# Rotary embedding: the first batch is stored in transfers of 8, 8 and 16 KB rows instead of four of 8 KB rows

## The chip, the core and the metric

The kernel runs on one core of a Trainium2 chip. The time is the device time of one execution in microseconds (us). The kernel before took 163.35 us, the median of three runs (163.34 to 163.67).

## What is computed

```python
x: [8, 2048, 8, 64] float32          # batch, sequence, heads, head dimension
cos, sin: [2048, 32] float32
x1, x2 = x[..., :32], x[..., 32:]
out1 = x1 * cos - x2 * sin           # cos, sin broadcast over batch and heads
out2 = x1 * sin + x2 * cos
out  = concatenate([out1, out2], axis=-1)
```

Each batch is 4 MB of input and 4 MB of output. With the two tables of 256 KB each, about 67.6 MB pass between HBM and SBUF.

## The kernel before

**Tiles.** The 2048 positions of a batch lie on 128 partitions, 16 positions on each, so one batch is one tile `xt` of 128 rows of 32 KB (`ROW` = 8192 floats). `UNIT` is a quarter of that, 2048 floats or 8 KB of each row. There are five such tiles (`NBUF = 5`); batches 5, 6 and 7 reuse the tiles of batches 0, 1 and 2. The result is written over the input in the same tile, and the tile is stored from there.

**Loads.** All loads of `x` are issued by SyncE (SP) in `load`, lines 64 to 70. Batch 0 comes in three transfers, with rows of 8, 8 and 16 KB; every other batch in one transfer with rows of 32 KB. The loads of batches 0 to 4 are issued at the start. The load of batch b+5 (line 193) stands behind the work of batch b and waits until every store of batch b has landed, because it overwrites that tile. Below, x0 to x7 are the loads of the batches.

**Stores.** `store`, lines 72 to 74, issues them on ScalarE's queue (ACT), for the last batch on SP's. `shares`, lines 177 to 182, says how a batch is cut into stores: batch 0 into four with rows of 8 KB (below s0a to s0d), batches 1 to 6 into one each (s1 to s6, rows of 32 KB), and the last batch into rows of 16, 8 and 8 KB (s7a to s7c). The loop at the end issues a store as soon as the pieces that it covers have been rotated.

**Arithmetic.** `rotate` works on pieces of `UNIT` floats of a row (the first and last of the work on half of that). In a piece of kind A, GpSimd (POOL) makes `t2` from the swapped halves and the sine table in two multiplications (line 122), VectorE (DVE) makes `t1` from `xt` and the cosine table (line 129) and adds both into `xt` (line 136). In the first pieces of batches 1 to 5 (kinds B and C) the addition is done by TensorE as two matmuls with the identity into PSUM, and ScalarE copies the sum into `xt` (lines 145, 165). In kind C, DVE also makes `t2` (line 148).

**What sets the order.** The order on each engine is that of the program (`keep_in_program_order`). On the two DMA queues that matter, q1 carries what SP issues and q10 what ACT issues. Each transfer announces its landing on one of eight semaphores that are handed out in turn, so a transfer may also have to wait for the landing of the one that had the same semaphore before it.

Of the kernel before, what the change touches and what calls it, by code (L numbers as in the profile page):

```python
# [10 lines left out]
def kernel(  # L11
# [18 lines left out]
    UNIT = 4 * HD  # L30
# [145 lines left out]

    def shares(b):
        if b == 0:
            return [UNIT] * 4
        if b == last:  # L180
            return [2 * UNIT, UNIT, UNIT]
        return [ROW]

    for b in range(B):
        done = 0
        outs = list(spans(shares(b)))
        for lo, n in spans(pieces(b)):
            rotate(b, lo, n)
            done = lo + n
            while outs and sum(outs[0]) <= done:  # L190
                store(b, *outs.pop(0))
        if b + NBUF <= last:
            load(b + NBUF)
# [30 lines left out]
```

## Time and profile before

| what | value |
|---|---|
| median of three runs | 163.35 us |
| the profiled execution, its own time | 164.17 us |
| its span, first to last instruction | 162.4 us |
| DVE busy | 140.1 us (86% of the span) |
| POOL busy | 138.8 us (85%) |
| PE, ACT busy | 49.1 us (30%), 12.8 us (8%) |
| DMA, moved in all | 67.65 MB, 417 GB/s over the span |
| q1, q10: share of the 16 DMA engines' time | 55.1%, 42.5% |

The profile is of one execution, 0.82 us above the median of the runs; 1.8 us of its time lie outside the span. Busy shares are of the whole span. In the digits by slice, each digit is a fortieth of the stretch shown, in tenths of full use, 9 being 90% or more. A transfer is spread over the 16 DMA engines: its 128 rows give 8 rows to each, and a record of a few bytes that marks the landing follows them on each engine. "To landing" is the time from a transfer's issue until the last of those marks.

### The profile page before, as it was taken

What the parts mean: (1) busy time and instruction counts of PE and PEld (TensorE: products, weight loads), DVE (VectorE), ACT (ScalarE), POOL (GpSimd) and SP (SyncE); (2) the same over time, 40 slices, a digit from 0 to 9 for tenths busy, and PEclk for the clock granted to TensorE, in tenths of its full rate; (3) what the DMA queues carried; (4) which work ended last, traced back from release to release, by engine and by line L of the source; (5) the groups of instructions that cost most, each with busy time, mean ns of one, the idle gap of its engine ahead of it and who ended that gap; (6) DMA issues with size and microseconds to landing.
All of it is one profiled execution on the core that took longest, in us unless ns stands there. A gap on an engine that the chain in (4) does not pass through costs nothing.

```text
span 162.4 us, 462 instructions
## 1 busy us (share of the span) xinstructions
PE 49.1 (30%) x80; PEld 18.5 (11%) x80; DVE 140.1 (86%) x66; ACT 12.8 (8%) x14; POOL 138.8 (85%) x70
## 2 busy tenths in 40 slices
PE   0000000597209750977058805971000000000000
PEld 0000000233003210322022302230000000000000
DVE  0397999999999999999999999999999999999300
ACT  3300000002200220022001120022000000000000
POOL 1499997999999999999995999999999999993000
PEclk9999999999965997589857995699555555555555
DMA  5999799899899899989999999899999999999992
GB/s 182 426 426 517 337 470 452 363 476 460 353 478 468 349 474 476 396 388 509 388 388 501 404 438 460 388 460 438 396 476 420 396 484 412 396 460 428 396 428 113
DMA packets 3602, 67.65 MB, mean 417 GB/s; under 512 B 400, under 2 KB 400, under 8 KB 656
## 3 DMA queue, kind: packets, MB, share of 16 engines
q1 hardware_dynamic: 2016, 38.01, 55.1%
q10 hardware_dynamic: 1584, 29.62, 42.5%
q14 instruction: 2, 0.02, 0.0%
HBM read 34.08 MB, written 33.55 MB: 417 GB/s over the span
## 4 chain that ended last, share of the span: by engine, by line
DVE 75%; POOL 9%; issue 6%; DMA 3%; DVEq 0%
DVE t L129 40%; DVE xt L136 33%; POOL t L122 9%; DMA sin_sb<-in_sin_dram 3%; DVE t L148 3%; DVEq L136 0%
## 5 line engine op out<-in xcount | busy, mean ns | idle before, releaser
L122 POOL TENSOR_TENSOR t<-xt,sin_sb 128x1024 f32<-128x1024 f32 (+1 forms) x32 | 70.7, 2210 | 8.2 <-DMA sin_sb<-in_sin_dram 5.0
L129 DVE TENSOR_TENSOR t<-xt,cos_ps 128x2048 f32<-128x2048 f32 (+1 forms) x34 | 73.4, 2166 | 0.8
L122 POOL TENSOR_TENSOR t<-xt,nsin 128x1024 f32<-128x1024 f32 (+1 forms) x32 | 70.7, 2211 | 0.0
L136 DVE TENSOR_TENSOR xt<-t,t 128x2048 f32<-128x2048 f32 (+1 forms) x29 | 62.2, 2145 | 4.2 <-POOL t L122 1.2
L143 PE MATMUL o<-t,eye 128*128 128x512 f32 x24 | 16.9, 794 | 23.2 <-DVE t L129 19.7
L160 PE MATMUL o<-t,eye 128*128 128x512 f32 x16 | 12.0, 842 | 37.6 <-DVE t L129 35.4
L144 PE MATMUL o<-t,eye 128*128 128x512 f32 x24 | 14.9, 709 | 0.0
L145 ACT COPY xt<-o 128x1024 f32<-128x1024 f32 x6 | 6.1, 1012 | 45.7 <-PE o L144 34.9
L143 PEld LDWEIGHTS o<-t,eye 128*128 128x128 f32 x24 | 5.6, 257 | 32.6 <-issue 26.7
L160 PEld LDWEIGHTS o<-t,eye 128*128 128x128 f32 x16 | 3.7, 257 | 43.1 <-issue 39.2
L165 ACT COPY xt<-o 128x1024 f32<-128x1024 f32 x4 | 4.0, 1012 | 47.7 <-PE o L161 47.7
L144 PEld LDWEIGHTS o<-t,eye 128*128 128x128 f32 x24 | 5.6, 235 | 8.0 <-issue 7.5
L93 DVE COPY cos_ps<-cos_sb 128x512 f32<-128x512 f32 x1 | 0.7, 695 | 6.8 <-DMA cos_sb<-in_cos_dram 6.8
L161 PE MATMUL o<-t,neye 128*128 128x512 f32 x8 | 6.2, 870 | 0.2
L148 DVE TENSOR_TENSOR t<-xt,sin_ps 128x2048 f32<-128x2048 f32 x2 | 4.6, 2280 | 0.0
L161 PE MATMUL o<-t,eye 128*128 128x512 f32 x8 | 4.1, 593 | 0.0
L161 PEld LDWEIGHTS o<-t,neye 128*128 128x128 f32 x8 | 2.1, 294 | 5.2 <-issue 3.6
L161 PEld LDWEIGHTS o<-t,eye 128*128 128x128 f32 x8 | 1.5, 190 | 1.9 <-issue 1.9
L90 ACT ACT_TABLE_LOAD x1 | 1.3, 1283 | 1.2 <-PEq L208 1.2
L90 ACT ACTIVATE nsin<-sin_sb 128x512 f32<-128x512 f32 x1 | 0.6, 629 | 3.9 <-DMA sin_sb<-in_sin_dram 3.9
L91 ACT COPY sin_ps<-sin_sb 128x512 f32<-128x512 f32 x1 | 0.6, 579 | 0.0
L80 POOL MEMSET eye<- 128x128 f32 x1 | 0.2, 206 | 0.3 <-POOLq L208 0.3
(6 smaller groups left out, 1.0 us busy)
## 6 DMA issues: line engine op xcount, KB each, us to landing
xt<-in_x_dram SPq DMA_DIRECT2D x7, 4096.0 KB, 27.9
out_dram<-xt ACTq DMA_DIRECT2D x6, 4096.0 KB, 34.0
out_dram<-xt ACTq DMA_DIRECT2D x4, 1024.0 KB, 26.5
xt<-in_x_dram SPq DMA_DIRECT2D x2, 1024.0 KB, 6.5
xt<-in_x_dram SPq DMA_DIRECT2D x1, 2048.0 KB, 12.0
out_dram<-xt SPq DMA_DIRECT2D x1, 2048.0 KB, 14.6
out_dram<-xt SPq DMA_DIRECT2D x2, 1024.0 KB, 10.9
sin_sb<-in_sin_dram ACTq DMA_DIRECT2D x1, 256.0 KB, 5.5
```

Source lines behind the costliest of these rows:

```text
L90: keep(nc.scalar.mul(nsin, sin_sb, -1.0))
L93: keep(nc.vector.tensor_copy(cos_ps, cos_sb))
L122: nc.gpsimd.tensor_mul(out=t2u[:, :, u, :].rearrange("p (r h) d -> p r h d", h=H), in0=xu[:, :, 1 - u, :].rearrange("p (r h) d -> p r h d" ...
L129: nc.vector.tensor_mul(out=t1.rearrange("p (r k d) -> p r k d", r=nr, d=Dh), in0=xk, in1=rep(cos_ps[:, r0 : r0 + nr, :], 2 * H),)
L136: keep(nc.vector.tensor_add(out=xt, in0=t1, in1=t2))
L143: nc.tensor.matmul(oc, eye, t1[:, cs], start=True, stop=False)
L144: nc.tensor.matmul(oc, eye, t2[:, cs], start=False, stop=True)
L145: keep(nc.scalar.copy(xt[:, 2 * j * C : 2 * (j + 1) * C], o))
L148: nc.vector.tensor_mul(out=t2.rearrange("p (r k d) -> p r k d", r=nr, d=Dh), in0=xk, in1=rep(sin_ps[:, r0 : r0 + nr, :], 2 * H),)
L160: nc.tensor.matmul(oc, eye, t1u[:, gs, u, :], start=True, stop=False)
L161: nc.tensor.matmul(oc, eye if u else neye, t2u[:, gs, 1 - u, :], start=False, stop=True)
L165: nc.scalar.copy(xu[:, :, u, :], o.rearrange("p (g d) -> p g d", d=Dh))
```

## The change

The third and the fourth quarter of batch 0 are stored by one transfer. It has 128 rows of 16 KB, is issued when the last piece of batch 0 is done, and carries 2 MB. The first two quarters are stored as before. Nothing else in the source changes.

```diff
     def shares(b):
         if b == 0:
-            return [UNIT] * 4
+            return [UNIT, UNIT, 2 * UNIT]
         if b == last:
             return [2 * UNIT, UNIT, UNIT]
         return [ROW]
```

In the built program ACT has one DMA instruction fewer: two stores of 128x2048 and one of 128x4096 stand where four of 128x2048 stood. The instructions of PE, DVE, POOL and SP, their order and their shapes are the same. As there is one transfer fewer, the semaphores that announce landings are handed out differently from there on. The load x2 then waits for the landing of the sine table instead of that of the first part of x0, x3 for the cosine table instead of the second part of x0, and x4 for the third part of x0 instead of the first store of batch 0.

## The prediction, made before the changed kernel was run

> **What bounds the kernel now.** I began with the page's rows by engine and by slice, because DVE (86%) and DMA both look full.
>
> ```profile
> span 162.4 us, 462 instructions
> ...
> DMA  5999799899899899989999999899999999999992
> ...
> DMA packets 3602, 67.65 MB, mean 417 GB/s; under 512 B 400, under 2 KB 400, under 8 KB 656
> ```
>
> The DMA digits are high from the second slice to the last but one. To see whether 9 means full, I asked for one stretch, from the first packet (1.7) to where DMA thins out (159.2); the last two columns are DMA share and GB/s.
>
> ```profile
> 1.70:159.20 157.50, 49.15 (x80) 18.53 (x80) 140.11 (x66) 12.22 (x14) 138.11 (x64) 0.77 1.00 429
> ```
>
> The share is 1.00: the 16 DMA engines never pause for 157.5 us. DVE in the same stretch is busy 140.1, and its last addition ends at 151.9, 10 us before the end. So the end is set by bytes, not by arithmetic. The tail shows by how much the DMA engines differ:
>
> ```profile
> DMA  8999995988999895331111111010100000000000
> ```
>
> Each digit is 0.135 us. At 159.2 nearly all engines are done; the ones are one or two engines that run on. Chaining the trace's packets engine by engine gives last ends of 159.2 to 159.8 on fourteen engines (median of all 16: 159.3), 160.64 on one and 161.13 on one. The span ends 1.2 us behind that last packet. The late engine carries the same rows; seven of its 32 KB rows took 1.28 to 1.72 us instead of 1.21, all between 66 and 125 us, and the second late one had an 8 KB instruction fetch of 0.31 followed by a row 0.54 too long.
>
> Next, who shares the engines while batch 0 is stored (42 to 62 us):
>
> ```profile
> q1 hardware_dynamic: 231, 6.52, 75.7%
> q10 hardware_dynamic: 245, 1.88, 22.2%
> ```
>
> Packets 231 to 245, bytes 3.5 to 1: an engine takes one row from each queue in turn, whatever its size. A store row of 8 KB gets one turn against a load row of 32 KB. Last, SP's waits and the issue of x5:
>
> ```profile
> SPq L67 <- DMA out_dram<-xt: 88.1, 4, 33.6
> ```
>
> ```profile
> 63.03 0.33 SPq L67 DMA_DIRECT2D xt<-in_x_dram  x1
> ```
>
> SP waits 33.6 us for batch 0's stores: s0d, issued at 27.6, needs 35.3 to land (62.9), and x5 goes out at 63.03.
>
> **The change, part by part.** I sum against the profiled execution (164.17, which is 0.82 above the median) and subtract the same from the median.
>
> *Saved transfer time.* In the packet records a row of 8 KB takes 0.309, of 16 KB 0.611, of 32 KB 1.213 us. Per engine, 8 x (2 x 0.309 - 0.611) = 0.056, and one landing mark fewer, 0.009: together 0.065 us off an engine that is never idle, so this counts in full. [...]
>
> *The ACT issue removed* (0.34 us) costs nothing: ACT next works at 36.78, and the joint store goes out at 27.6.
>
> *The third quarter waits longer*, from 22.9 to 27.6. That is covered by q10's own backlog: the first rows of the four stores run at 17.1, 29.4, 41.6 and 53.7, every 8 x (1.213 + 0.309) = 12.2 us, so until 41.6 the queue has s0a and s0b to serve. Were it empty, the 4.7 us would show (third rival).
>
> *The new semaphore order* moves the issue of x3 from 9.3 to about 6.8 and of x4 from 28.9 to about 14.2 (landings 6.7 and 14.1), and of x2 from 6.1 to 6.3. Their rows run at 37.7, 49.8 and 25.4, one load behind the other on q1, so all are issued long before their turn: nothing.
>
> *The joint store.* From 41.6 its 8 rows alternate with 8 load rows: 8 x (1.213 + 0.611) = 14.6, to 56.2; with the mark and its way about 56.8. Batch 0's tile is free 6.1 us earlier than 62.9, and SP issues x5 at about 57 instead of 63. But q1 is then not empty. Of x3 and x4, 8 rows pass in those 14.6 us (in the profile nearly 10), and 5 rows of x4 are left. They now alternate with s1's 32 KB rows: 5 x 2.43 = 12.1, to about 68.5. There x5 begins, where in the profile it began at 67.1. Between 61.6 and 67.1 q1 was empty in the profile, and s1 had the engines alone; that gap is filled, no bytes are gained. From there on both queues stay full, loads are one pair of rows (2.4 us) later than before and stores one pair earlier:
>
> x5 lands at 87.0 + 2.4 = 89.4; POOL wants it at 97.05. x6 lands at 106.7 + 2.4 = 109.1; wanted at 110.79. x7 lands at 126.3 + 2.4 = 128.7; wanted at 129.05. s1 and s2 land at about 76.4 and 96.7 instead of 78.8 and 99.1, so x6 and x7 are issued earlier, which changes nothing, as they queue behind x5 and x6. The thinnest cover is x7's:
>
> ```profile
> 129.05 2.32 POOL L122 TENSOR_TENSOR t<-xt,sin_sb 128x1024 f32<-128x1024 f32 x1
> ```
>
> If x7 is d late for that, POOL's pair of operations ends at 133.65 + d, and DVE adds at 134.96: 1.3 more. If DVE slips too, the last store (issued at 151.9) still has the engines' backlog: its first row runs at 156.7, and by the nearest row, s7a's 3.8 us from issue to first row, it could be issued 1.0 later. So 0.35 + 1.3 + 1.0 = 2.6 us cover x7, and I charge nothing.
>
> *The lag of the slowest engine* is the unknown. It was 161.13 - 159.3 = 1.8 us and grew where load rows of 32 KB alternate with store rows of 32 KB. From below: without it the end is 159.8, the next engine's, so up to 1.4 us are to be won. From above: 29 load rows per engine now meet 32 KB store rows instead of 24 (the five of x4 join), which scaled gives 1.8 x 29/24 = 2.2, or +0.4; one more fetch of the observed kind on the late engine would add 0.31 + 0.54. I take 0, since neither seed of the lag is visibly removed or doubled for certain, and keep -1.4 to +0.85 for the range.
>
> Sum: 164.17 - 0.065 + 0 = 164.1 for the profiled execution, 163.35 - 0.065 = 163.3 for the median.
>
> **Rivals.** A measurement of this kernel can tell about 0.2% (0.33 us) from no change, so "same" is 163.02 to 163.68.
>
> *Slower: the lag grows.* The stretch of 32 KB against 32 KB rows lengthens as above. For: all but one of the late engine's long rows fell in that stretch, three of them right behind a store's landing mark, and one more such mark (s0c's) now falls among loads. Against: the marks at 28, 40 and 52 us, between 8 KB store rows, left the next load row at its usual length. It decides when the late engine gains over 0.4 us; with +0.4 to +0.85 the time is 163.7 to 164.2.
>
> *Faster: the lag shrinks.* The late engine's first long row (0.22 too long) ran at 66.2, the last before x5 came up on the empty queue. That restart vanishes. If that engine then keeps step, the other one is last: 160.64 - 161.13 = -0.5, or 162.8; if both do, -1.4, or 161.9. Against: the restart as cause rests on one row.
>
> *Slower: the joined store starts late and pushes x5, x6, x7.* The third store's 4.7 us are then paid: x5 first at 71.7, x7 landing at 130.9, 1.9 behind POOL's wish, 0.6 left for DVE, and at most that at the end: 163.9 at worst. It needs an empty q10 at 22.9, where s0b was issued at 18.2 and took 22.8 to land, so it has 3 in 100. [...]
>
> *The usual hope, that x5's earlier issue speeds the kernel,* is in my sum: x5 starts later, not earlier.
>
> **The numbers.** No change 0.37; lag grows 0.30 and late store 0.03, so slower 0.33; lag shrinks 0.30. The likeliest is no change, 163.3 (163.0 to 163.7 by itself). The range leaves out about 1 in 10 on each side: below, the case where both late engines keep step; above, a lag grown by more than 0.85: 162.5 to 164.2.
>
> **What would show it.** Right: DMA share 1.00 up to about 159; s0c lands near 56.8; x5 is issued near 57 but lands near 89, later than before; x7 near 128.7; s1 near 76.4; DVE ends at 151.9. Wrong: a gap in the DMA share, x5 landing before 87, POOL waiting for x7 by over 2.6 us, or last packet ends that differ from 161.1 while the median engine stays at 159.3, which would put the change into the lag.

## The result and the profile after

In 20 runs each the changed kernel took 163.40 us (163.29 to 163.53) and the kernel before 164.14 (163.34 to 165.46): ratio 0.996, interval 0.9945 to 0.9974. It is 0.4% faster, a little over the 0.2% that I had called the bound. The three runs known beforehand (median 163.35) lay at the low end of a wide spread; the profiled execution of before, 164.17, was the typical one. The change narrows the spread from 2.1 to 0.24 us, and takes the median down to near the best that the kernel before reached.

The page and the same stretch as before (its last two columns are DMA share and GB/s), both of the changed kernel:

```profile
span 161.5 us, 460 instructions
...
DMA  5999998998999999999999999999999999999994
...
DMA packets 3458, 67.65 MB, mean 419 GB/s; under 512 B 384, under 2 KB 384, under 8 KB 640
```

```profile
1.70:159.40 157.70, 49.24 (x80) 18.53 (x80) 140.11 (x66) 12.22 (x14) 138.22 (x64) 0.77 1.00 429
```

The same bytes, the same full share, the same DVE time. What differs is the end. DMA share from 157 us on after the change, each digit 0.135 us; the same row of the kernel before, shown in the prediction, reaches six digits further, with eleven digits from 1 to 3 behind its fall where this one has three (1, 2, 1): a few of the sixteen engines were still at work there:

```profile
DMA  7795959898594979851020100000000000000000
```

The median DMA engine ends at 159.33 before and at 159.52 after, so the common work got no shorter. (In the profile after, the rows of x1 already ran 0.25 us later at 15 us, before any store.) The last engine ends at 161.13 before and at 160.36 after: 0.77 of the 0.82 us between the two profiled executions (164.17 and 163.35). Measured from the median engine, the last one lags by 1.80 us before and by 0.84 after. In all profiles of this study the whole time is the last engine's end plus 2.9 to 3.2 us, so these last ends stand for the times.

The steps in the middle are there much as worked out. The queues from 42 to 62 us (packets, MB, share of the engines), SP's waits, the issue of x5, and POOL's first operation on x7:

```profile
q1 hardware_dynamic: 176, 5.24, 61.8%
q10 hardware_dynamic: 177, 3.42, 39.8%
```

```profile
SPq L67 <- DMA out_dram<-xt: 79.0, 4, 26.9
```

```profile
55.98 0.33 SPq L67 DMA_DIRECT2D xt<-in_x_dram  x1
```

```profile
129.43 2.32 POOL L122 TENSOR_TENSOR t<-xt,sin_sb 128x1024 f32<-128x1024 f32 x1
```

Packets are equal in number again, and the share of the stores' queue rose from 22% to 40%. The last 6 us of that stretch are 32 KB rows of s1 already; from 42 to 54 us, where batch 0's rows run, its share is 36% after and 20.5% before. s0c, issued at 27.92, lands 28.0 us later, at 55.9; x5 goes out at once, 7 us earlier than before, and lands 33.8 us later, at 89.8, so 2.8 us later than before. x7 lands at 129.30, 0.13 us ahead of POOL.

### The profile page after: what moved, and what is told of

The parts are those of the page before. It is cut to its first block, busy times and chain, and to the rows that moved or that the text cites. A ratio compares the mean times of both kernels' runs of the same rounds, so it can differ in the third digit from the quotient of the medians.

```text
span 161.5 us, 460 instructions
## 1 busy us (share of the span) xinstructions
PE 49.2 (30%) x80; PEld 18.5 (11%) x80; DVE 140.1 (87%) x66; ACT 12.8 (8%) x14; POOL 138.9 (86%) x70
## 4 chain that ended last, share of the span: by engine, by line
DVE 75%; POOL 9%; issue 6%; DMA 4%; DVEq 0%
DVE t L129 40%; DVE xt L136 33%; POOL t L122 9%; DMA sin_sb<-in_sin_dram 4%; DVE t L148 3%; DVEq L136 0%
```

## The experiments

Theory 1 was that the late engine comes from the pause of q1 (61.6 to 67.1 us before the change, filled by the change). Theory 2: it comes from the number and the row sizes of batch 0's stores, by a way not known. Theory 3, in the first four: chance of the runs; in the later ones: x4's earlier issue, which the new semaphore order brings. Theory 5 is theory 1 refined after the eighth run (there is no 4). "Late engine" is one whose packets end behind those of the engines that have an instruction fetch. A "long" row is one that took more than its usual time (1.213 us for 32 KB). For each version the median time is given, with the lowest and the highest run, and then its ratio to the kernel before on the same chip, with a 95% interval.

**The kernel before, again** (no edit).

> The kernel before once more, for a second profile of it. Theory 1 (the pause: q1 runs empty from 61.6 to 67.1 us while s1 has the DMA engines alone, and when x5 starts against it, single engines fall out of step and stay late): the time is that of before within 0.2%, the spread of its runs over 1 us, and one or two DMA engines end 1.5 us or more behind the median engine, their long rows beginning at or after 66 us. Theory 2 (the number and size of the store rows of batch 0 and the order of semaphores that goes with it): the same, but long rows may begin before 62 us. Theory 3 (chance of the runs): a second profile shows no late engine but those with an instruction fetch.

163.99 us (163.68 to 164.30), ratio 0.9989 (0.9965 to 1.0014). In its profile the engines split at the end of the pause: five take x5's first row between 67.2 and 67.7 us, eleven first begin one more row of s1 and take x5's at 68.2 to 68.6. At 77 us the five have load rows of 1.9 to 2.4 us instead of 1.21 (those of the eleven take 1.3 to 1.6), and the last ends come at 160.9. So not one late engine, but a late group; the place fits theory 1.

**The 16 KB rows first.**

```diff
-            return [UNIT] * 4
+            return [2 * UNIT, UNIT, UNIT]
```

> Batch 0 in three stores again, but with the 16 KB rows first (16, 8, 8). Number of transfers, row sizes and semaphore order as in the changed kernel, but the last store of batch 0 still goes in 8 KB rows behind the others: by the row times 22 + 14.6 + 2 x 12.2, so it should land at about 62, and q1 runs empty as before. Theory 1: as the kernel before, ratio 1.000 within 0.002, a late engine again. Theory 2: as the changed kernel, ratio 0.996, spread of the runs 0.3 us.

163.65 (163.55 to 163.83), 0.9979 (0.9959 to 0.9999): between the two. One premise was wrong: batch 0 landed at 62.7 as worked out, but x4 only at 66.5, so q1 did not run empty. Its own loss lies elsewhere: near 22 us, where the first 16 KB rows come up against x1, load rows on all engines are long, by 0.77 us per engine from 14 to 42 us. The versions with 8, 8 and 16 KB rows have less, but are not free of them: 0.28 to 0.65 us up to 54 us (0.32 in the changed kernel), half or more of it near 40 and 50 us.

**x4 in two halves.**

```diff
-        for lo, n in spans([UNIT, UNIT, 2 * UNIT] if b == 0 else [ROW]):
+        for lo, n in spans([UNIT, UNIT, 2 * UNIT] if b == 0 else [2 * UNIT] * 2 if b == 4 else [ROW]):
```

> Stores as before the change (four with 8 KB rows), but the load x4 in two transfers with 16 KB rows. From 49.8 us a turn then takes 0.611 + 0.309 instead of 1.213 + 0.309, so batch 0 should have landed at about 61, with five 16 KB rows of x4 left, which end near 69: q1 does not run empty. One transfer more than before. Theory 1: as the changed kernel, ratio 0.996 (0.994 to 0.998), spread of the runs 0.3 us, last DMA engine within 1 us of the median engine. Theory 2: as the kernel before, 1.000 within 0.002.

163.72 (163.51 to 165.02), 0.9997 (0.9965 to 1.0028). q1 stays filled (x5 issued at 59.95, x4's second half lands at 70.8), and yet five of twelve runs are above 164. Against theory 1.

**The changed kernel with x5 held back.**

```diff
         xt = xpool.tile([P, ROW], f32, tag="xt", name=f"xt{b}")
+        if b == 5:
+            keep(nc.vector.memset(xt[:, 0:1], 0.0))
...
+        if (b, lo) == (3, UNIT):   # in rotate, ahead of the addition
+            load(5)
+            load(6)
...
-        if b + NBUF <= last:       # behind each batch's work
-            load(b + NBUF)
+        if b == 3:
+            load(7)
```

> The changed kernel, with x5 held back: DVE writes one column of x5's tile behind its first multiplication of batch 3's second piece, at about 69 us, and the load waits for that (0.1 us of DVE). x4 ends at about 70, so q1 runs empty for some 3 us, as it does before the change for 5.5. x7 then lands some 2 us later, which POOL and the queue's backlog should cover to within 0.3 us. Theory 1: the late engine is back, ratio 0.999 to 1.002, spread of the runs over 0.8 us. Theory 2: as the changed kernel, 0.996 to 0.998, spread 0.3 us.

163.31 (163.25 to 164.80), 0.9964 (0.9939 to 0.9988); eleven of twelve runs are 163.68 or less. The edit missed its aim: x4 ended later too (it landed at 72.4), and only three store rows ran between its landing mark and x5, where the changed kernel has one. The profile is of the one run of 164.80; there one engine was late by long load rows at 24, 37, 41 and 56 us already.

**Two stores of 16 KB rows.**

```diff
-            return [UNIT] * 4
+            return [2 * UNIT, 2 * UNIT]
```

> Batch 0 in two stores with 16 KB rows, one transfer fewer than the changed kernel. By the row times batch 0 lands at about 53 and q1 never runs empty. Theory 1 (q1's pause makes the late engine): ratio 0.994 to 0.998, no long rows between 66 and 90 us beside those of an instruction fetch. Theory 2 (fewer and larger rows of batch 0): at least as fast as the changed kernel, 0.996 or less. Were only the transfer's row overhead at work, it would be 0.06 us below the changed kernel.

163.60 (163.47 to 164.05), 0.998 (0.9969 to 0.9991). Slower than the changed kernel, so fewer and larger is not the rule; it has the same long rows near 22 us (0.73 us per engine) as the 16, 8, 8 division. Its last store was issued at 155.94, 4 us later than before the change; its first row ran 1.1 us later, and no engine had paused for it.

**Two pieces left unrotated** (the control).

```diff
+        if b == last and lo in (2 * UNIT, 3 * UNIT):
+            return                 # at the head of rotate, in the changed kernel
```

> The changed kernel with the third and fourth piece of the last batch left unrotated (they are stored as loaded), so DVE has 7.2 us less to do at the end and all bytes still move. The control for the next run. If bytes set the end: 0.995 to 0.997, as the changed kernel, with DVE ending near 145. If DVE set it: 5 us or more faster (ratio under 0.97).

163.37 (163.29 to 163.59), 0.9962 (0.9946 to 0.9978). The rows by stretch (columns PE, PEld, DVE, ACT, POOL, clock, DMA share, GB/s) show the last 7 us of DVE's work gone and the DMA share as it was:

```profile
130.00:145.00 15.00, 0.00 (x0) 0.00 (x0) 14.13 (x8) 0.00 (x0) 11.08 (x6) 0.50 1.01 435
145.00:152.00 7.00, 0.00 (x0) 0.00 (x0) 0.00 (x0) 0.00 (x0) 0.00 (x0) 0.50 0.97 419
```

Bytes set the end, and not DVE; that is shown.

**The pause put back** (the control's edit, and x5 held as in the fourth run, but behind the addition of batch 3's second piece).

> As the run before it (the same two pieces left unrotated), with x5 held back by a column that DVE writes into its tile behind batch 3's second piece, at about 72 us. x4's rows end at 70.5, x5's begin near 76: q1 is empty for some 5 us, as in the kernel before the change. x6 and x7 land some 5 us later and DVE with them, which the two left-out pieces cover. Theory 1: long rows come back on single engines between 74 and 100 us, the last engine ends 1.3 us or more behind the median one, time 0.5 to 0.8 us above the run before it (ratio 0.999 to 1.001 against the kernel before). Theory 2: as the run before it, 0.995 to 0.997.

163.43 (163.26 to 164.10), 0.9977 (0.9965 to 0.9988). x5 was issued at 71.62, and its first rows run at 75.8 to 76.1 on all sixteen engines, 5.8 us behind x4's last landing mark. No engine split off, and from 54 us on no row was long by over 0.1 us but those behind the fetches; the tail is short, with the two engines of the instruction fetches last:

```profile
DMA  9897999999598989951110100000000000000000
```

The pause by itself does not bring the loss back (three of the twelve runs do lie above all of the control's, one at 164.10). Theory 1 as first put has fallen.

**The last quarter on SP's queue.**

```diff
-        queue = nc.sync if b == last else nc.scalar
+        queue = nc.sync if b == last or (b == 0 and lo == 3 * UNIT) else nc.scalar
...
-    for b in range(NBUF):
+    for b in range(NBUF - 1):     # load(4) then follows batch 0's last store
```

(The stores are those of before the change.)

> Four stores with 8 KB rows as before the change, but the fourth is issued on SP's queue, ahead of x4. It runs at about 50 us between x3 and x4 instead of at 53.7 behind the third store, batch 0 has landed near 54, x5 is issued then, and x4 ends near 70: q1 does not run empty, with the number of transfers and the row sizes as before. Theory 1: 0.994 to 0.998, as the changed kernel. Theory 2: as the kernel before, 1.000 within 0.002.

167.51 (167.26 to 167.82), ratio 1.0223 (1.0204 to 1.0241). I had overlooked that s1 was already waiting in q10: from 51.4 us each 8 KB row of s0d took its turn behind a 32 KB row of s1. s0d landed at 60.7 instead of 54 and x4 at 80.7; POOL, free at 72.1, began batch 4 only then. x5 landed at 100.9, 1.7 us after POOL was free for it (3.9 us after POOL had begun it in the profile before), and x7 at 139.4. DVE waited for POOL and POOL for loads (us, times, longest):

```profile
DVE xt L136 <- POOL t L122: 10.8, 6, 4.7
```

It says nothing on the late engine, but gives the price of late loads: DVE ends 9.2 us later than before, and the last packet 3.5.

**x4 issued late in the changed kernel.**

```diff
+        if b == 4:
+            keep(nc.vector.memset(xt[:, 0:1], 0.0))   # in load
...
-    for b in range(NBUF):
+    for b in range(NBUF - 1):
...
+        if b == 0:                 # behind each batch's work
+            load(NBUF - 1)
```

> The changed kernel, with the load x4 issued as late as before the change (about 28 us instead of 14.4): DVE writes one column of x4's tile when batch 0 is rotated, and the load waits for it. Takes the change of the semaphore order back and leaves the stores. Theory 3 (x4's early issue, from the new semaphore order, is what counts): as the kernel before, 0.999 to 1.001. Theory 5 (the restart of q1: when x5 comes up against s1 at the moment at which some engines end a row and others have just begun one, the engines split into two groups, one row apart, and those that are late stay late; in the changed kernel x5 is in the queue in time and nothing restarts): as the changed kernel, 0.995 to 0.997, 163.4 us, spread 0.3 us.

163.37 (163.29 to 163.51), 0.9959 (0.9939 to 0.9979), with x4 issued at 27.9. Theory 3 has fallen: x4's early issue is not what counts.

**The kernel before with x5 held back** (the edit of the fourth run).

> The kernel before, its four 8 KB stores and its semaphore order kept, but x5 held back by a column that DVE writes into its tile at about 69 us. The pause of q1 grows from 5.5 to some 11 us. The restart is then set by DVE's time and no longer by the landing of s0d on the last engine, which is also what begins s1's rows, so it falls between rows of different engines only by chance. Theory 5: faster than before although x5 comes 6 us later: 0.995 to 0.998, most runs within 163.3 to 163.7 and one or two in twelve above 164. Theories 2 and 3 (rows and transfers of batch 0; semaphore order): as before, 0.999 to 1.001. Theory 1 as first put (the pause itself): as before or slower, 1.000 to 1.004.

163.59 (163.23 to 164.18), 0.997 (0.9942 to 0.9998). x5 came 6 us later than before the change, and the kernel was not slower, probably faster, as theory 5 had it; eight of its twelve runs are above all but one of the control's. In its profile fifteen engines begin x5 between 73.3 and 73.6 us; the sixteenth had just begun a row of s2 (73.38), which took 1.67 us; it then had long load rows and ended last, at 160.58.

**The kernel before, a third profile** (no edit).

> The kernel before a third time, one profile. Theory 5: at x5's first row near 67 us the engines either split into groups one row apart, and the last engine ends at 160.7 or later with long rows between 66 and 100 us, or they all take x5 at the same row, and the last end is 160.4 or less. Theories 2 and 3 have no tie between the two.

164.07. Two engines, the last two in phase, were in a row of s1 begun at 66.32 and 66.35 when x5 arrived; the rows took 0.14 and 0.35 us too long, and the second had a load row 0.66 too long at 78.8. Their ends are 160.38 and 161.04. With the first profile (0.22 at 66.17, end 161.13) this made three of three for theory 5.

**The pause filled.**

```diff
     for b in range(NBUF):
         load(b)
+    fill = const_pool.tile([P, 128], f32, tag="fill")
+    keep(nc.sync.dma_start(out=fill, in_=xv[0, :, 0:128]))
```

(In the kernel before the change.)

> The kernel before, with one small load more on SP's queue behind x4: 128 rows of 512 B from x into a tile that nothing reads (64 KB, 0.15 us of the 16 engines). Its eight rows and its mark take turns with s1's 32 KB rows from about 62 to 71 us, so q1 is not empty when x5 arrives, and x5's first row comes near 71 instead of 67. Stores, their rows and their order stay as before the change; there is one transfer more. Theory 5 (the restart of q1): 163.4 to 163.7, ratio 0.996 to 0.998, spread of the runs 0.4 us, no long row near 66 us and no engine behind those with an instruction fetch. Theory 2 (rows and number of batch 0's stores): as before or slower by the bytes, 1.000 to 1.002.

164.21 (163.57 to 164.80), ratio 1.0014 (0.9996 to 1.0032). The filler worked: q1's small rows alternate with s1's until 69.7 and x5 follows from 70.9 on, with no restart. Yet from 67 to 90 us rows are long on nearly all engines (0.22 us on average), on one of them by 1.37 in all, and that engine ends at 161.69:

```profile
DMA  7999599898999799794302020111001010000000
```

Theory 5, as the cause, has fallen too: an engine can fall behind without q1 having run empty.

**What the runs leave.** Grouped by how batch 0 is stored. The last two columns are from the profiles, one execution of each version: the end of the median DMA engine, and how far the last one lags behind it. (The last row's two columns also have the first and the third profile of the kernel before.)

| stores of batch 0 (KB rows) | versions | medians, us | runs above 163.9 | median engine ends | last engine lags |
|---|---|---|---|---|---|
| 8, 8, 16 | changed kernel; x5 held; control; pause back; x4 late | 163.31 to 163.43 | 2 of 66 | 159.5 to 159.7 | 0.7 to 0.8, once 2.1 (the run of 164.80) |
| 16, 8, 8 and 16, 16 | two | 163.65, 163.60 | 1 of 24 | 159.95, 159.87 | 0.8, 0.6 |
| 8, 8, 8, 8 | before, again; x4 in halves; x5 held; filler | 163.59 to 164.21 | 22 of 48 | 159.3 to 159.8 | 0.8 to 2.1 |

The run with the last quarter on SP's queue is left out, as DVE and the loads set its end.

What is shown: in the two profiles of before and after, the gain is the late engine, not the common work. The late engine, and with it the wide spread, goes with the four 8 KB stores (22 of 48 runs, and 13 of the 20 of the kernel before in the result) and is rare with fewer stores (3 of 90), whether x4 is issued early or late, whether q1 pauses or not, and whether DVE has time to spare. The two versions that begin with 16 KB rows have no late engine either. By their profiles they lose their 0.2 us against the changed kernel in the common work: their median engine ends later, which fits the long rows near 22 us.

The four-quarter versions fall behind in different places (a split at the restart, single long rows, a burst at 74 to 80 us). One regularity stands in the packet records: of their five profiles with a late engine, four (first, third, x5 held, filler) have a long store row on that engine which ran just as x5's first rows began on the others (from 66.17, 66.35, 73.38 and 69.96 us). In the profiles of the changed kernel and of x4 in halves, which have no late engine, the rows at that place took their usual time. That says where the engine begins to fall behind, not why. Why the four 8 KB stores leave the rows from 66 us on open to this, and fewer stores do not, stays open. No run tells the number of the stores from the size of their rows or from the earlier issue of the third quarter, so I can't say which of these counts. Of the versions run, none was measurably faster than the changed kernel.

## Why the prediction was right or wrong

*That bytes set the end and DVE does not*: right, shown by the control (7 us of DVE's work gone, 163.37 us against 163.40).

*The saved transfer time, 0.065 us*: too small to be seen. The median engine ended 0.19 us later, and 0.25 us of difference stood between the two executions at 15 us already.

*The order of the queues*: right to about a microsecond. s0c landed at 55.9 (56.8 forecast), x5 was issued at 56.0 (57) and landed at 89.8 (89.4), x6 at 109.9 (109.1), x7 at 129.3 (128.7), s1 at 75.2 (76.4). That x5's earlier issue brings a later x5 held. One step of it was short: x5's first rows were forecast at about 68.5, 1.4 us behind the profile before, and still 2.4 us were charged. They ran at 71.0, because x4's last row is followed by two rows of s1, with x4's landing mark taking q1's turn between them. The tables came 0.3 us later in this execution, and with them POOL's wish for x7, so the 0.35 us of cover were 0.13.

*No cost for the ACT issue and the semaphore order*: of the second, x4's part is shown by the run with x4 late; the rest was not tested.

*The cover of x7, 2.6 us*: too small. The 1.0 us for the last store came from s7a's 3.8 us from issue to first row, a row under full load. With two stores of 16 KB the last store was issued 4.0 us later than before, and no engine paused. In the run with the last quarter on SP's queue DVE ended 8.9 us later than in the changed kernel and the last packet 4.2, so some 4.7 us were covered there.

*The lag of the slowest engine*: the step that failed. I took 0 for this term, with -1.4 to +0.85 as its bounds. Between the two profiles the lag behind the median engine went from 1.80 to 0.84, so the term measured -0.96; with the median engine's +0.19 the last end moved by -0.77, and the medians of the runs by -0.74. With it the outcome was that of the rival "the lag shrinks" (0.30), not of the likeliest case (0.37). Its reason, that the restart of q1 vanishes, was not borne out: filling the pause left the lag, putting the pause back did not bring it. The rival "the lag grows" argued that 29 pairs of 32 KB rows do more than 24; there were those pairs, and no late engine.

*163.3 us against 163.40 measured*: right by luck. The base, 163.35, was the median of three runs at the low end of before's spread; from the typical 164.14 the same sum would have given 164.1, 0.7 us too much. A base that was too low hid a term that was missing. I noted that the profiled execution lay 0.82 above the median and did not ask what that says of the spread.

## What to carry to other kernels

In a kernel bound by bytes, look at where each DMA engine ends, not only at their mean share: here nearly all of the change (0.77 of 0.82 us between the two profiles) was in the last of sixteen. A single execution 0.5% above the median of three is a sign that the time has a spread, which can be the very thing that a change moves. And before an order of transfers is judged by when a transfer is issued, count the rows that stand ahead of it in its own queue: x5 was issued 7 us earlier and landed 2.8 us later.

## What the runs showed of the hardware

In the records of this case an engine takes one row from each of the two queues in turn. From 42 to 62 us it is 231 packets of q1 (rows of 32 KB and marks) against 245 of q10 (rows of 8 KB and marks) before the change, and 176 against 177 after it, where q10 has rows of 16 and then of 32 KB. The filler's eight rows of 512 B on each engine (0.02 us each) held q1 open for eight rows of s1 of 1.21 us. A landing mark (0.009 us) takes a turn of its own.

Each of the fourteen profiles has two 8 KB instruction fetches on DMA engines, at 90 to 100 and at 110 to 125 us. Each takes 0.31 us. The row behind the first is 0.53 us too long in twelve of the fourteen, the row behind the second 0.22 in all. In the profiles of the changed kernel, the control, the pause put back and x4 late, nothing else makes an engine late from 54 us on: the 0.84 us of the first fetch are about what separates their last engine from the median one (0.68 to 0.84).
